# An interleaved attention pipeline: value loads asked for two turns ahead, bank-freeing steps first, new keys in the score bank

## The chip, the cores and the metric

The kernel runs on one core of a Trainium2 chip. TensorE (PE) multiplies matrices: a weight load (PEld) puts the stationary operand in place, a matmul streams the other one and writes PSUM, which has eight banks of 512 fp32 columns for each of the 128 partitions. VectorE (DVE), ScalarE (ACT) and GpSimd (POOL) do the elementwise work, and SyncE (SP) issues the DMAs to and from HBM. Each engine takes its instructions in order and waits on semaphores that other engines raise. The metric is the time of one launch on the device in microseconds.

## The reference, cut to what matters

Two layers of a streaming encoder are computed for a prompt of 512 frames and for 8 running streams of 16 frames each, 640 rows in all. Layer 0 has a feed-forward block (`ffn0`), a mixer of a complex state-space model beside stick-breaking attention (`mix0`), and a second feed-forward block; layer 1 has an SSD mixer between two feed-forward blocks. The change is inside the attention of `mix0`:

```python
def sb_block(q_blk, q_pos, k, v):
    z = jnp.einsum('bqhd,bkhd->bhqk', q_blk, k).astype(jnp.float32) * (SB_HEAD_DIM ** -0.5)
    mask = k_pos[None, :] < q_pos[:, None]
    sp = jnp.where(mask, jax.nn.softplus(z), 0.0)
    suffix = lax.cumsum(sp, axis=3, reverse=True) - sp
    w = jnp.where(mask, jnp.exp(jax.nn.log_sigmoid(z) - suffix), 0.0)
    return jnp.einsum('bhqk,bkhd->bqhd', w, v)
...
out = jnp.concatenate([s5_out, sb_out], axis=-1) @ w_out
```

There are 8 heads of 64. A prompt row sees the prompt rows before it; a row of a running stream sees 256 cached keys and values of its stream and the new rows before it.

## The kernel before, in words

**Units and turns.** The 8 heads go in four pairs `p`. Each pair has four units `u`: three cut up the prompt's causal triangle (`parts_of`, 512 or 384 score columns for each head), and `u == 3` is the running streams (384 columns: 128 of new keys, 256 of cached ones). The 16 units run as a pipeline of 16 turns, one unit a turn, in the loop `for s, (p, u) in enumerate(units)`. I number the turns 0 to 15, so turn 4p + u belongs to unit (p, u).

**What one unit needs.** `score` multiplies queries by keys into `z`, a PSUM tile of two banks (L1222, the mask by L1227; for the streams L1234, L1236 and L1239). `soft` on ACT makes softplus in three passes (L1246, then L83 twice). `sums` on DVE adds (L1256), runs the suffix sum as a scan (L1263) and subtracts (L1265). `expo` on ACT takes the exponential (L83 on `S`). `turn` on PE transposes the weights back into the same banks `z` (L1275), ACT copies them out to `es` (L1361), and `product` multiplies by the values (L1285; for the streams L1299 with the new values `vrev` and L1303 with the cached values `vc`). In turn `s` stand `turn(s)`, the copy L1361 of unit s, `expo(s + 1)`, `product(s)`, then `begin(s + 2)`, which gives `score(s + 2)`, then `soft(s + 2)` and `sums(s + 2)`. There are two `z` tiles.

**New keys.** The streams' score needs the pair's 128 new keys in reversed order. `new_keys(p)`, called by `begin` of unit (p, 1), takes a bank of the pool `a`, transposes the keys into it (L1203), copies them out (L1202), multiplies by a reversing matrix into the same bank (L1206) and copies that out (L1207), which ends in `kr[p]`.

**Values.** For unit (p, 3) `product` asks for four tiles `vc` of 256 KB, two for each half `f`, right at the matmuls that use them. There are three buffers.

**Fill.** Between the attention's own matmuls PE is given other work of the mixer: the projections of queries and keys of the next pairs, the gate of the state-space part and the first half of the output projection. They are `Group`s of 12 or 24 matmuls (L1021), each into one of three banks of the pool `a`. `fill(1.8)` stands between `turn` and `product`, `fill(3.2)` at the end of a turn; the figures are planned microseconds. A group starts only when the group three before it has been read out (`held[-3]`); before the change a `new_keys` counted as one of those holders. What reads a bank out are ACT steps (L1109 for queries and keys) or DVE steps (L1148 for the gate, L1184 for the output).

**Side work of ACT and DVE.** Steps that wait for their place are `Job`s in two lists. `slot(engine, us)` takes jobs that are ready from the front of the list until `us` is used up: casts of weights into a high and a low part (L1085, L1088), copies of activations into such parts (L1122, L1123), the gate's sigmoid (L83 on `gs`) and the readings of banks.

**What fixes the order.** From the mark before the pipeline to its end every PE, ACT and DVE instruction is chained to the one before it on its engine, so these three run in the order in which the code gives them. DMAs are not chained; the SP queue is laid out when the program is built. After the last turn the groups that are left run to their end, and then `out_half(4, t)` (L134) does the second half of the output projection.

## Time and profile before

| | |
|---|---|
| median of three runs | 2596.32 us (2596.07 to 2597.92) |
| the profiled execution's own time | 2597.03 us |
| its span, mean granted clock of PE | 2595.3 us, 0.988 |
| busy share of PEld, DVE, ACT, POOL | 89%, 78%, 47%, 11% |
| HBM traffic, mean over the span | 116 GB/s |
| the pipeline of 16 turns, with the groups left at its end | 568.65 to 757.97 us |
| `vc` loads: count, size, median time to landing | 16, 256 KB, 4.1 us |

A row of the timeline has the start, the duration, the engine, the line, the operation, what it writes and reads, the shape and how many instructions it merges; in brackets stands how long the engine was idle before it and what ended that. A row of the waits has the waiting engine, tile and line, what it waited for, then the total, the number of times and the longest. In a row of windows PEclk is the TensorE clock that was granted, as a share of full speed. Everything outside these 189 us is the same before and after the change.

### The profile page before, as it was taken

What the parts mean: (1) busy time and instruction counts of PE and PEld (TensorE: products, weight loads), DVE (VectorE), ACT (ScalarE), POOL (GpSimd) and SP (SyncE); (2) the same over time, 40 slices, a digit from 0 to 9 for tenths busy, and PEclk for the clock granted to TensorE, in tenths of its full rate; (3) what the DMA queues carried; (4) which work ended last, traced back from release to release, by engine and by line L of the source; (5) the groups of instructions that cost most, each with busy time, mean ns of one, the idle gap of its engine ahead of it and who ended that gap; (6) DMA issues with size and microseconds to landing.
All of it is one profiled execution on the core that took longest, in us unless ns stands there. A gap on an engine that the chain in (4) does not pass through costs nothing. (4 is left out here: it accounts for less than half of the span.)

```text
span 2595.3 us, 40664 instructions
## 1 busy us (share of the span) xinstructions
PE 2520.8 (97%) x15577; PEld 2303.1 (89%) x15577; DVE 2018.7 (78%) x3685; ACT 1226.3 (47%) x2329; POOL 285.4 (11%) x412
## 2 busy tenths in 40 slices
PE   8999999999799999999999999999999999999998
PEld 8999999878578999998999999889999878999997
DVE  7788877765657988887888887777777698876768
ACT  4443344346634454554355554566565443443332
POOL 0000002110011000003000001411111151000001
PEclk9999999999899999999999999999999999999999
DMA  5332334543211244443144335356564622443442
GB/s 181 106 106 81 115 111 140 169 134 108 87 53 49 66 126 110 110 126 107 57 110 115 106 93 164 89 181 182 179 199 136 232 95 77 153 153 113 142 137 94
DMA packets 174835, 317.44 MB, mean 122 GB/s; under 512 B 20480, under 2 KB 91776, under 8 KB 174128
## 3 DMA queue, kind: packets, MB, share of 16 engines
q1 hardware_dynamic: 164816, 293.83, 35.7%
q0 software_dynamic: 9824, 21.01, 3.9%
q8 instruction: 122, 2.00, 0.3%
q14 instruction: 73, 0.60, 0.1%
HBM read 259.56 MB, written 40.54 MB: 116 GB/s over the span
## 5 line engine op out<-in xcount | busy, mean ns | idle before, releaser
L96 DVE TENSOR_TENSOR w<-raw,w 128x512 fp32r<-128x512 f32 (+1 forms) x601 | 525.4, 899 | 78.3 <-ACT w L95 76.6
L95 ACT CAST w<-raw 128x512 fp32r<-128x512 f32 (+1 forms) x601 | 442.0, 776 | 297.1 <-PE bank L134 107.4
L356 PE MATMUL bank<-xhi,w 128*128 128x320 f32 x2432 | 540.1, 309 | 1.7 <-ACT mx L367 1.4
L134 PE MATMUL bank<-xhi,w 128*128 128x256 f32 (+2 forms) x2272 | 500.0, 312 | 14.5 <-ACT xhi L95 8.4
L134 PE MATMUL bank<-w,h 128*128 128x512 f32 x1872 | 435.3, 391 | 0.2 <-DVE w L96 0.2
L356 PE MATMUL bank<-T,w 128*128 128x320 f32 x2736 | 426.2, 309 | 2.0 <-DVE s L393 1.7
L134 PEld LDWEIGHTS bank<-w,h 128*128 128x128 f32 x1872 | 349.2, 188 | 72.9 <-DVE h L96 1.0
L356 PEld LDWEIGHTS bank<-xhi,w 128*128 128x128 f32 x2432 | 407.3, 188 | 5.9 <-ACT mx L367 2.8
L356 PEld LDWEIGHTS bank<-T,w 128*128 128x128 f32 x2736 | 406.4, 188 | 3.9 <-DVE s L393 2.2
L134 PEld LDWEIGHTS bank<-xhi,w 128*128 128x128 f32 x2272 | 379.6, 189 | 26.0 <-ACT xhi L95 9.6
L356 PE MATMUL bank<-xlo,w 128*128 128x320 f32 x1216 | 375.0, 308 | 0.0
L134 PE MATMUL bank<-xlo,w 128*128 128x256 f32 (+2 forms) x1136 | 351.9, 310 | 5.7 <-DVE xlo L96 5.7
L356 PEld LDWEIGHTS bank<-xlo,w 128*128 128x128 f32 x1216 | 228.0, 188 | 0.3
L134 PEld LDWEIGHTS bank<-xlo,w 128*128 128x128 f32 x1136 | 214.6, 189 | 7.6 <-DVE xlo L96 6.8
L209 DVE SCALAR_TENSOR_TENSOR yacc<-bank,yacc 128x512 f32<-128x512 f32 x160 | 109.4, 687 | 77.3 <-PE bank L134 76.7
L367 ACT COPY mx<-bank 128x320 f32<-128x320 f32 x228 | 96.3, 423 | 141.4 <-PE bank L356 140.6
L96 DVE TENSOR_TENSOR w<-sw,w 128x1024 fp32r<-128x1024 f32 x76 | 93.0, 1224 | 53.1 <-ACT w L95 52.8
L95 ACT CAST w<-sw 128x1024 fp32r<-128x1024 f32 x76 | 79.8, 1050 | 100.3 <-DVE sw L335 99.1
L500 POOL DMA_DIRECT2D yacc<-ev x56 | 48.6, 884 | 652.8 <-ACT ev L499 594.6
L134 PE MATMUL bank<-w,og 128*128 128x512 f32 x432 | 106.2, 400 | 3.5 <-DVE og L1769 3.5
L134 PEld LDWEIGHTS bank<-w,og 128*128 128x128 f32 x432 | 80.8, 191 | 21.5 <-DVE og L1769 5.1
L395 ACT ACTIVATE s<-s 128x320 f32<-128x320 f32 x108 | 50.8, 471 | 85.2 <-DVE s L393 85.0
(428 smaller groups left out, 3487.5 us busy)
## 6 DMA issues: line engine op xcount, KB each, us to landing
raw<-in_w_gate_dram SPq DMA_DIRECT2D x88, 512.0 KB, 3.8
raw<-in_w_up_dram SPq DMA_DIRECT2D x88, 512.0 KB, 4.0
raw<-in_w_down_dram SPq DMA_DIRECT2D x88, 512.0 KB, 3.6
raw<-in_m_in_dram SPq DMA_DIRECT2D x52, 512.0 KB, 4.6
yacc<-ev POOLq DMA_DIRECT2D x56, 256.0 KB, 4.1
raw<-in_m_out_dram SPq DMA_DIRECT2D x24, 512.0 KB, 3.8
csb<-cs_d SPq DMA_DIRECT2D x20, 512.0 KB, 5.0
h<-in_ssd_h_dram SPq DMA_DIRECT2D x16, 512.0 KB, 6.0
```

What stands on the lines that cost most here:

```text
L95: nc.scalar.copy(hi, src)
L96: return nc.vector.tensor_tensor(lo, src, hi.bitcast(F32), op=ALU.subtract)
L134: state["pe"] = nc.tensor.matmul(ps, a, b, start=(k == 0), stop=(k == n - 1)).ins
L209: state["acc"] = nc.vector.scalar_tensor_tensor(ya, pb, scale, ya, op0=ALU.mult, op1=ALU.add).ins
L356: nc.tensor.matmul(ps, A[p][:, a, k * 128:k * 128 + 128], B[p][b][:, k, :], start=(first and n == 0), stop=(n == 11), skip_group_check=True)
L367: nc.scalar.copy(e[n], ps)
L395: state["silu"] = nc.scalar.activation(t, ps, AF.Silu).ins
L500: nc.gpsimd.dma_start(yacc[:, t, 512 * j:512 * j + 512], e, accum_op=ALU.add)
```

## The change

1. The four `vc` tiles of unit (p, 3) are asked for in `begin` of that unit, which stands two turns ahead of its `product`, into four buffers instead of three.
2. Jobs that free a bank (what `Group.then` returns, and the first copy of the new keys) get `frees`, and `slot` takes these first.
3. `new_keys(p, z)` uses the 128 columns of each of unit (p, 1)'s two score banks that its 384 score columns leave over, instead of a bank of pool `a`: the transposition (now L1200) goes to columns 384 to 511 of the first, the reversed keys (now L1205) to those of the second. The copies are now L1201 and L1206. New keys no longer count among the holders of pool `a`.
4. The first `slot("act", 1.9)` of a turn becomes 2.6, the second 1.2.

```diff
@@ -964,7 +964,7 @@
             class Job:
 
                 def __init__(self, cost, give, needs=()):
-                    self.cost, self.give, self.needs, self.done = cost, give, list(needs), False
+                    self.cost, self.give, self.needs, self.done, self.frees = cost, give, list(needs), False, False
 
                 def ready(self):
                     return all(n.done for n in self.needs)
@@ -987,7 +987,7 @@
             def slot(engine, us):
 
                 while us > 0:
-                    todo[engine] = [j for j in todo[engine] if not j.done]
+                    todo[engine] = sorted((j for j in todo[engine] if not j.done), key=lambda j: not j.frees)
                     j = next((j for j in todo[engine] if j.ready()), None)
                     if j is None:
                         return
@@ -1022,6 +1022,7 @@
                                      skip_group_check=True)
                     if not self.left:
                         self.freed = self.then(self.ps)
+                        self.freed.frees = True
 
                 def run(self):
                     while not self.done:
@@ -1190,25 +1191,22 @@
 
             units = [(p, u) for p in range(4) for u in range(4)]
             parts_of = (((3, 0),), ((2, 0),), ((1, 0), (0, 256)))
-            ch, kr, po = {}, {}, {}
+            ch, kr, po, vals = {}, {}, {}, {}
             qbf = qb.rearrange("p f b h i -> p f (b h i)")
 
-            def new_keys(p):
+            def new_keys(p, z):
 
                 kk = wk.tile([128, 2, 128], F32, name="kk", bufs=2)
-                if len(held) > 2 and not held[-3].freed.done:
-                    held[-3].freed.run()
-                pk = bank_a()
-                first = later("act", 0.25, lambda: nc.scalar.copy(kk[:, 0], pk[:, 0:128]))
-                nc.tensor.transpose(pk[:, 0:128], qk[p, "k"][:, 512:640], ident)
+                nc.tensor.transpose(z[:, 0, 384:512], qk[p, "k"][:, 512:640], ident)
+                first = later("act", 0.25, lambda: nc.scalar.copy(kk[:, 0], z[:, 0, 384:512]))
+                first.frees = True
 
                 def turned():
-                    nc.tensor.matmul(pk[:, 128:256], kk[:, 0], anti, start=True, stop=True)
-                    nc.scalar.copy(kk[:, 1], pk[:, 128:256])
+                    nc.tensor.matmul(z[:, 1, 384:512], kk[:, 0], anti, start=True, stop=True)
+                    nc.scalar.copy(kk[:, 1], z[:, 1, 384:512])
 
                 kr[p] = Job(0.25, turned, [first])
-                kr[p].keys, kr[p].freed = kk[:, 1], kr[p]
-                held.append(kr[p])
+                kr[p].keys = kk[:, 1]
 
             def score(s):
                 p, u = units[s]
@@ -1238,6 +1236,8 @@
                         for j in range(4):
                             nc.tensor.matmul(z[32 * j:32 * j + 32, f, 128:384], qbf[:, f, 32 * j:32 * j + 32],
                                              kc[:, j, :], start=False, stop=(j == 3), skip_group_check=True)
+                if u == 1:
+                    new_keys(p, z)
                 ch[s] = [z[:, :, :n], wk.tile([128, 2, 512], F32, name="es", bufs=3)[:, :, :n], None]
 
             def soft(s):
@@ -1290,11 +1290,7 @@
                 wT = e.rearrange("p f (k r) -> p f k r", k=3)
                 ps = po[p, "s"] = bank("o")
                 for f in range(2):
-                    vcs = []
-                    for k in range(2):
-                        vc = wk.tile([128, 4, 128], F32, name="vc", bufs=3)
-                        nc.sync.dma_start(vc, I["vc"][p][:, 4 * f:4 * f + 4, k])
-                        vcs.append(vc)
+                    vcs = vals[p][2 * f:2 * f + 2]
                     o = slice(128 * f, 128 * f + 128)
                     nc.tensor.matmul(ps[:, o], wT[:, f, 0], vrev[:, 128 * p:128 * p + 128],
                                      start=(f == 0), stop=False, skip_group_check=True)
@@ -1325,13 +1321,17 @@
                             if p:
                                 made[p, n, h].run()
                 if u == 1:
-                    new_keys(p)
                     for h in range(2):
                         rows = slice(64 * h, 64 * h + 64)
                         nc.gpsimd.tensor_copy(qb[rows, :, :, h, :],
                                               qk[p, "q"][rows, 512:640].rearrange("p (f b i) -> p f b i", f=2, i=16))
-                if u == 3 and not kr[p].done:
-                    kr[p].run()
+                if u == 3:
+                    vals[p] = [wk.tile([128, 4, 128], F32, name="vc", bufs=4) for _ in range(4)]
+                    for f in range(2):
+                        for k in range(2):
+                            nc.sync.dma_start(vals[p][2 * f + k], I["vc"][p][:, 4 * f:4 * f + 4, k])
+                    if not kr[p].done:
+                        kr[p].run()
                 score(s)
 
             for p in (1, 2, 3):
@@ -1359,7 +1359,7 @@
                     fetch(order[len(raws)])
                 turn(s)
                 nc.scalar.copy(ch[s][1], ch[s][0])
-                slot("act", 1.9)
+                slot("act", 2.6)
                 fill(FILL[0])
                 if s + 1 < len(units):
                     expo(s + 1)
@@ -1381,7 +1381,7 @@
                     sums(s + 2)
                 if u == 0:
                     kr[p].run()
-                slot("act", 1.9)
+                slot("act", 1.2)
                 fill(FILL[1])
                 if (p, u) == (3, 2):
                     split_x(7, qk[3, "q"], 0, TP, [made[3, n, h] for n in "qk" for h in range(2)])
```

Lines below line 1190 move up by two to four: L1222, L1227, L1239, L1303 and L1184 are L1220, L1225, L1237, L1299 and L1185 in the changed program; those near L1100 move down by one.

**SP, the loads around the pair p = 1.** `raw` are weights, `kc` cached keys, `out_kT` a result. Before:

```order
L1075 DMA raw<-in_m_out_dram 128x1024 x2
L1233 DMA kc<-in_kcT_dram 128x1024 x2
L1111 DMA out_kT_dram<-kT 128x640
L1075 DMA raw<-in_m_out_dram 128x1024
L1296 DMA vc<-in_vc_dram 128x4x128 x2
```

After:

```order
L1231 DMA kc<-in_kcT_dram 128x1024 x2
L1112 DMA out_kT_dram<-kT 128x640
L1076 DMA raw<-in_m_out_dram 128x1024
L1332 DMA vc<-in_vc_dram 128x4x128 x3
L1076 DMA raw<-in_m_out_dram 128x1024
L1332 DMA vc<-in_vc_dram 128x4x128
```

Before, the two `vc` at this place are the fourth of pair 0 and the first of pair 1, each behind the matmuls that free one of the three buffers; after, the `vc` at this place are all four of pair 1.

**PE, around the first transposition (turn 0).** Before:

```order
L1021 MATMUL bank<-xlo,w 128x256
L1275 MATMUL bank<-ident,S 128x128 x8
L1285 MATMUL bank<-es,vt 64x128 x8
L1222 MATMUL bank<-kT,qT 128x256 x2
L1222 MATMUL bank<-kT,qT 128x128 x2
```

After:

```order
L1021 MATMUL bank<-xlo,w 128x384
L1021 MATMUL bank<-xhi,w 128x384
L1275 MATMUL bank<-ident,S 128x128 x8
L1021 MATMUL bank<-xhi,w 128x384
L1021 MATMUL bank<-xlo,w 128x384
```

A third group of 24 matmuls of 384 columns now starts here, since no new keys hold a bank: 10 of them stand ahead of the transposition and 11 between it and the product.

**ACT, from the softplus of unit (2, 1) to the copy of turn 8.** Before (the copies of the new keys are L1202 and L1207):

```order
L1246 ACTIVATE es<-bank 128x2x384
L83 ACTIVATE es<-es 128x2x384 x2
L1122 CAST xhi<-g_4561 128x384
L1122 CAST xhi<-g_4562 128x384
L1122 CAST xhi<-g_4563 128x384
L1122 CAST xhi<-g_4564 128x384
L1361 COPY es<-bank 128x1024
```

After:

```order
L1246 ACTIVATE es<-bank 128x2x384
L83 ACTIVATE es<-es 128x2x384 x2
L1201 COPY kk<-bank 128x128
L83 ACTIVATE gs<-gs 128x256 x3
L1361 COPY es<-bank 128x1024
```

The first copy of the new keys now stands ahead of the copy L1361 of turn 8, with a sigmoid (`gs`) between. It reads a bank that DVE reads too, and in the changed program it waits for DVE's subtraction L1265 on that bank (for the pairs 1 to 3; for pair 0 it stands ahead of DVE's pass). The matmul L1205 has the same wait, for all four pairs.

**ACT, from the softplus of unit (2, 3) to the copy of turn 10, after the change:**

```order
L1246 ACTIVATE es<-bank 128x2x384
L95 CAST w<-raw 128x512
L83 ACTIVATE es<-es 128x2x384
L95 CAST w<-raw 128x512
L83 ACTIVATE es<-es 128x2x384
L1123 CAST xhi<-g_4563 128x256
L1123 CAST xhi<-g_4564 128x256
L83 ACTIVATE gs<-gs 128x384 x3
L1361 COPY es<-bank 128x2x384
```

Before, six sigmoid steps of 256 columns stood between the last pass of the softplus and the copy of this turn, and no cast.

## The prediction

> **What bounds the kernel now.** I read the page's first two parts first, then windows around the 16 turns, then PE's waits there, then the timelines of the turns in which it waits.
>
> ```profile
> span 2595.3 us, 40664 instructions
> PE 2520.8 (97%) x15577; PEld 2303.1 (89%) x15577; DVE 2018.7 (78%) x3685; ACT 1226.3 (47%) x2329; POOL 285.4 (11%) x412
> ```
>
> PE is busy for 97% of the span, so only its 75 us of idle time and the time at a low clock can be won without taking work away. The windows below take the pipeline as a whole and then in three parts, turns 0 to 6, turns 7 (its end) to 12, and the rest.
>
> ```profile
> core 0: us, PE busy (x) PEld busy (x) DVE busy (x) ACT busy (x) POOL busy (x), PEclk, DMA share, GB/s
> 568.65:757.97 189.32, 159.76 (x1119) 127.55 (x1118) 106.54 (x156) 109.41 (x178) 2.90 (x8) 0.89 0.26 81
> 568.65:652.41 83.76, 77.58 (x596) 65.14 (x595) 48.08 (x62) 52.26 (x79) 1.16 (x4) 0.94 0.31 100
> 652.41:718.68 66.27, 47.67 (x317) 36.43 (x318) 39.73 (x64) 44.50 (x77) 0.58 (x2) 0.79 0.28 84
> 718.68:757.97 39.29, 34.52 (x208) 25.98 (x206) 18.74 (x32) 12.65 (x23) 1.16 (x2) 0.96 0.10 36
> ```
>
> The pipeline takes 189.3 us. PE is idle for 189.3 - 159.8 = 29.6 us of it, and a mean clock of 0.89 loses up to 0.11 x 189.3 = 20.8 us more (5.0, 13.9 and 1.6 by its three parts; what of it falls on idle time costs nothing). The middle part is the worst, with 18.6 us idle. No other engine is full there: ACT has 44.5 of 66.3 us, DVE 39.7. So PE waits for answers, not for an engine's throughput.
>
> ```profile
> PE bank L1303 <- DMA vc<-in_vc_dram: 10.3, 4, 4.1
> PE bank L1285 <- ACT es L1361: 6.0, 3, 4.0
> PE bank L1021 <- ACT kT L1109: 4.1, 1, 4.1
> PE bank L1206 <- ACT kk L1202: 2.8, 1, 2.8
> PE bank L1275 <- ACT S L83: 2.5, 1, 2.5
> PE bank L1021 <- DVE yacc L1184: 1.2, 1, 1.2
> PE bank L134 <- DVE yacc L1184: 1.2, 1, 1.2
> PE bank L1021 <- DVE gs L1148: 0.6, 1, 0.6
> PE bank L1311 <- ACT pvs L1307: 0.5, 1, 0.5
> PE bank L1299 <- ACT es L1361: 0.4, 1, 0.4
> ```
>
> These ten rows add up to the 29.6 us.
>
> **Part 1, the values: 10.3 us go.** The last eight matmuls of each streams' product wait for a load.
>
> ```profile
> 695.49 5.81 SPq L1296 DMA_DIRECT2D vc<-in_vc_dram  x4
> 700.21 0.66 PE L1303 MATMUL bank<-vc,es 128*32 128x128 f32 x8 [4.12 <-DMA vc<-in_vc_dram]
> ```
>
> With three buffers the fourth tile can be asked for only when the product has read the first one, and part of the load (4.1 us to landing, the median of the 16) then lies bare on PE. With four buffers all four are asked for once the previous pair's product is through, some 30 us ahead; the two results and weight loads that stand before them on SP wait for steps of earlier turns. Nothing is late in their place: the cached keys have had their buffers before. All 10.3 us go.
>
> **Part 2, banks: the other 19.3 us go, some comes back.** A third group starts early, and readings of banks come first. In turn 0:
>
> ```profile
> 581.48 1.10 PE L1275 MATMUL bank<-ident,S 128*128 128x128 f32 x8 [2.49 <-ACT S L83]
> 583.67 1.97 PE L1285 MATMUL bank<-es,vt 128*64 128x128 f32 x16 [1.10 <-ACT es L1361]
> 590.25 0.51 PE L1021 MATMUL bank<-xhi,w 128*128 128x384 f32 x2
> 590.77 0.51 PE L1021 MATMUL bank<-xhi,w 128*128 128x384 f32 x2
> ```
>
> Three matmuls of 384 columns take 0.52 us start to start, so ten ahead of the transposition cover 1.7 us of the first wait and eleven behind it the whole second one; about 1.0 us is left. The wait for L1109 (4.1) goes, since that step no longer stands behind four copies; the one for L1206 (2.8) goes, since the copy it waits for now stands ahead of an L1361 that PE has waited for by then. The waits for DVE's `yacc` (2.4) go: five matmuls are left at the end instead of 51, and the bank of the first L134 has then long been read. The product's waits in turns 9 and 12 (4.9 of the 6.0) are priced anew in parts 3 and 4.
>
> **Part 3, the new keys: a new wait for ACT.** No row of before shows ACT waiting with the copy of the keys, for they had a bank of their own. In the program after, L1201 waits for L1265, DVE's last pass over the score bank; behind it in ACT's queue stands L1361, for which PE's product waits. The nearest rows are those of turn 4:
>
> ```profile
> 616.90 0.39 PE L1227 MATMUL bank<-negc,identb 128*128 128x128 bf16 x2
> 617.33 0.81 ACT L1246 ACTIVATE es<-bank 128x768 f32<-128x768 f32 x1 [1.11 <-PE bank L1227]
> 618.17 1.72 ACT L83 ACTIVATE es<-es 128x768 f32<-128x768 f32 x2
> 620.06 0.26 ACT L1202 COPY kk<-bank 128x128 f32<-128x128 f32 x1
> 619.92 0.96 DVE L1256 SCALAR_TENSOR_TENSOR es<-bank,es 128x768 f32<-128x768 f32 x1 [1.50 <-ACT es L83]
> 622.76 0.96 DVE L1265 TENSOR_TENSOR S<-bank,S 128x768 f32<-128x768 f32 x1
> 622.00 1.04 PE L1275 MATMUL bank<-ident,S 128*128 128x128 f32 x8
> 623.07 1.02 ACT L1361 COPY es<-bank 128x1024 f32<-128x1024 f32 x1 [2.75 <-PE bank L1275]
> ```
>
> From the score's end to the end of L1361 it will be 2.6 (three passes of ACT) + 3.8 (619.92 to 623.72 on DVE) + 0.26 + 1.02 + about 0.3 of hand-overs = 7.9 us. Meanwhile PE has streams_back with a wait for `pvs` (0.8), the fill of 3.2 planned (19 matmuls, 3.3), the transposition (0.8) and the fill of 1.8 planned (1.9): 6.8. So turn 4 waits 1.2 us. In turn 8 a sigmoid of three passes stands between (1.25) and only two matmuls fill between transposition and product (0.35): 7.9 + 1.25 - 5.4 = 3.8. In turn 12 two copies stand between (1.2): 7.9 + 1.2 - 6.8 = 2.3. Sum **7.3**. Bounds: nothing, if PE is late for other reasons and the pass is over; 3 x (3.8 + 0.26 + 1.0) = 15.2, if all of pass and copies lies bare. I take the middle, which the rows of turn 4 give.
>
> **Part 4, ACT's jobs in turns 9 and 10.** More sigmoids and casts stand ahead of the copy for the product than before.
>
> ```profile
> 681.71 2.51 ACT L83 ACTIVATE gs<-gs 128x256 f32<-128x256 f32 x6
> 690.56 0.60 ACT L95 CAST w<-raw 128x512 fp32r<-128x512 f32 x1
> 694.10 0.71 ACT L1122 CAST xhi<-g 128x256 fp32r<-128x256 f32 x2
> 717.15 1.64 ACT L83 ACTIVATE gs<-gs 128x384 f32<-128x384 f32 x3
> 684.12 0.78 ACT L1361 COPY es<-bank 128x768 f32<-128x768 f32 x1
> 710.40 1.98 PE L1285 MATMUL bank<-es,vt 128*64 128x128 f32 x16 [3.99 <-ACT es L1361]
> ```
>
> Turn 10: from the score's end 2.6 + two casts 1.2 + two copies 0.7 + a sigmoid 1.64 + L1361 0.8 = 6.9; PE has six matmuls (1.05) and the transposition (0.6), as no further group can start: it waits 5.3. Turn 9: 2.6 + 1.2 + 0.25 (second copy of keys) + 2.5 + 0.8 = 7.3 against 0.2 + 3.3 + 0.6 + 1.9 = 6.0: it waits 1.3. Sum **6.6**; bounds nothing and 6.9 + 7.3 = 14.2. The last row shows such a wait in turn 12 of before (3.99), of the same kind. The larger first `slot` (2.6 for 1.9) stands behind L1361 of its own turn and ahead of the next exponential, which PE needs only some 5 us later; I price it at nothing (at most 16 x 0.7 = 11 us if that cover went).
>
> **The sum.** Idle: 29.6 goes; 7.3 + 6.6 + 1.0 (turn 0) + 2.0 (four waits for `pvs`, 0.5 each as in the row of L1311) + 0.6 (DVE's bank readings, as now) = 17.5 comes: 12.1 saved. The matmuls moved forward from the end are no saving of their own, they fill this. Clock: in the middle part 13.9 us are lost beside 18.6 idle, 0.75 for each idle us; by that rate the five new stalls and turn 0, 13.9 + 1.0 = 14.9 us, lose 11.2 instead of 20.5: 9.3 saved. Together 21.4 us off the profiled execution's own 2597.0 (span and what lies around it), which is 0.7 over the median of the runs: **2575 us** as a median, 0.8% less.
>
> **A rule on the clock.**
>
> ```profile
> 615.35 0.42 PE L1303 MATMUL bank<-vc,es 128*32 128x128 f32 x8 [2.08 <-DMA vc<-in_vc_dram]
> 617.00:618.00 1.00, 1.00 (x6) 0.50 0.94 357
> 620.00:621.00 1.00, 1.00 (x7) 0.96 0.00 0
> ```
>
> A stall of 2.08 us was followed by half clock from about 616.8 to 620.1, 3.3 us, or 1.6 us lost. The Trainium skill ("TensorE: Matmul & The Clock Gate", Part 1) says the clock halves after an idle window of some 3.4 us, in windows that run freely. The window's length agrees with the trace, the idle time needed doesn't: 2.08 us were enough.
>
> **Rivals.**
>
> *A, only long stalls cost clock.* If just the two longest stalls (turns 8 and 10, 3.8 and 5.3) halve it, for one window of 3.3 us each, 3.3 us are lost instead of 11.2: 2567 us. For it: turns 0 to 6 lose only 5.0 us of clock. Against: the 2.08 above. The Trainium skill, on the page and in the part named above, gives a limit of some 3.4 us, which lies between 2.08 and 3.8.
>
> *B, the chain of answers was the bound, not the banks.* A turn cannot be shorter than score, softplus, DVE's pass, exponential, transposition and copy let it; matmuls put between then only hide what was hidden, and the product waits as long as before. Then only the values' 10.3 us are won: 2586 us. For it: ACT and DVE hand over five times within a turn. Against: turns 0 to 6 have 83.8 - 77.6 = 6.2 us idle, turn 0's 3.6 and one load's 2.1 among them, so the other turns run without a wait where there is fill.
>
> *C, slower.* The hold of L1201 blocks ACT in turns 4, 8 and 12 and delays the score behind the product, so the next softplus and DVE's pass start late and the delay rolls on through turns 9 to 13. Each us of stall costs 1.75 with its clock, so the sign turns once the five stalls (turns 4, 8, 9, 10, 12) together exceed 13.9 + 21.4 / 1.75 = 26 us, 5.2 each. At 6.5 each they are 18.6 over my sum, and the time is 2575 + 33 = 2608 us. For it: in the program after, the wait is on the whole of DVE's pass, not on the columns that are read. Against: ACT has a third of that part free (44.5 of 66.3). The Trainium skill ("PSUM — Partial Sum Buffer", PSUM bank collisions raise a hardware error) says that two engines must not be at one bank and quadrant together even at different columns, two readers included; so by it the spare columns can't be read while DVE is at the bank; no run here shows a collision.
>
> *D, the loads come no earlier.* SP works in order; were the values to stay behind a weight load that waits for its buffer, the 10.3 us and some 5 of clock would stay: 2590 us. Against: the order, in which they stand behind steps of earlier turns.
>
> **How the numbers follow.** Forecast 0.57, A 0.13, B 0.14, C 0.07, D 0.05; within 0.2% of before (5 us, about what a measurement of this kernel can tell from no change) 0.04 more. Faster gathers the forecast, A, B and most of D: 0.87; the same 0.06; slower 0.07. The unknown prices move the forecast by 7.3 + 6.6 = 14 downwards (no such stall, 2561) and by 7.9 + 7.6 = 15 upwards (2590), so the range of 2561 to 2590 takes in A, B and D and leaves out C.
>
> **What would show it.** The waits of L1303 for a DMA: none. The first L1275: 1.0 us of wait. L1201 idle before it for 3 us or more in three turns, released by L1265. The product of turn 10 waiting about 5 us, turn 8 about 4. Five matmuls L1021 between L1307 and L134. A mean clock of 0.93 to 0.94 over the pipeline, which is about 168 us long. Wrong would be a wait for `vc` left, product waits over 20 us together, or a pipeline over 180 us.

## The result, and the profile after

The changed kernel takes **2571.62 us** (median of 4 runs, 2568.28 to 2576.97), against 2597.12 us (2596.07 to 2599.11, 4 runs) of the kernel before on the same chip: a ratio of 0.9903, 95% interval 0.9884 to 0.9922. Forecast were 2575 us. The profiled execution took 2573.02 us, 24.0 less than the profiled one of before.

The first rows are the span and the engines from the page; then the windows, the pipeline as a whole and its three parts with turns 0 to 6, the middle, and the rest (columns as in the rows of before).

```profile
span 2571.3 us, 40672 instructions
PE 2511.2 (98%) x15577; PEld 2297.1 (89%) x15577; DVE 2017.1 (78%) x3685; ACT 1225.1 (48%) x2329; POOL 287.3 (11%) x412
```

```profile
572.02:736.34 164.32, 148.06 (x1120) 119.54 (x1119) 107.04 (x155) 108.28 (x175) 3.35 (x8) 0.96 0.28 87
572.02:652.41 80.39, 77.15 (x637) 65.17 (x636) 49.78 (x66) 55.06 (x86) 1.16 (x4) 1.00 0.35 115
652.41:713.41 61.00, 48.74 (x324) 37.91 (x325) 42.70 (x68) 43.15 (x75) 1.03 (x2) 0.89 0.26 78
713.41:736.34 22.93, 22.17 (x163) 16.46 (x161) 14.56 (x23) 10.06 (x15) 1.16 (x2) 1.00 0.05 14
```

The pipeline is 25.0 us shorter (189.3 to 164.3). Two terms make this up: PE is idle for 164.3 - 148.1 = 16.3 us of it instead of 29.6, which is 13.3 less, and the same matmuls keep it busy for 148.1 instead of 159.8, which is 11.7 less, since more of them run at full clock. Ahead of the pipeline this execution lost 3.4 us (it starts at 572.02, before at 568.65), which the last section takes up. Behind it it won 2.4; this I did not follow up, but the two executions of one kernel below, e10_no_frees and c2_no_frees, differ there by 4.7 us (1839.7 and 1835.0 us from the pipeline's end to the span's), so it is no more than chance makes.

PE's waits in the pipeline, first all of them, then one by one from the timeline:

```profile
PE bank L1285 <- ACT es L1361: 12.9, 5, 4.9
PE bank L1307 <- ACT pvs L1303: 1.1, 2, 0.6
PE bank L1275 <- ACT S L83: 1.0, 1, 1.0
PE bank L1021 <- ACT kT L1110: 0.6, 1, 0.6
PE bank L1275 <- ACT kk L1206: 0.4, 1, 0.4
PE bank L1021 <- DVE yacc L1185: 0.3, 1, 0.3
```

```profile
584.85 1.09 PE L1275 MATMUL bank<-ident,S 128*128 128x128 f32 x8 [1.00 <-ACT S L83]
624.31 0.88 PE L1285 MATMUL bank<-es,vt 128*64 128x128 f32 x12 [1.01 <-ACT es L1361]
662.47 1.97 PE L1285 MATMUL bank<-es,vt 128*64 128x128 f32 x16 [4.01 <-ACT es L1361]
673.66 0.88 PE L1285 MATMUL bank<-es,vt 128*64 128x128 f32 x12 [0.66 <-ACT es L1361]
683.39 1.55 PE L1285 MATMUL bank<-es,vt 128*64 128x128 f32 x12 [4.87 <-ACT es L1361]
706.00 1.58 PE L1285 MATMUL bank<-es,vt 128*64 128x128 f32 x16 [2.35 <-ACT es L1361]
```

No row waits for a load any more. What is left is nearly all the product's wait for L1361, in turns 4, 8, 9, 10 and 12. In turn 8 the timelines of ACT, and under it of DVE, show why:

```profile
655.34 0.85 ACT L83 ACTIVATE es<-es 128x768 f32<-128x768 f32 x1
660.04 0.27 ACT L1201 COPY kk<-bank 128x128 f32<-128x128 f32 x1 [3.85 <-DVE S L1265]
660.21 1.31 ACT L83 ACTIVATE gs<-gs 128x256 f32<-128x256 f32 x3
661.43 0.99 ACT L1361 COPY es<-bank 128x1024 f32<-128x1024 f32 x1
```

```profile
656.22 0.96 DVE L1256 SCALAR_TENSOR_TENSOR es<-bank,es 128x768 f32<-128x768 f32 x1 [0.32 <-ACT es L83]
657.21 1.81 DVE L1263 TENSOR_TENSOR_SCAN S<-onec,es 128x384 f32<-128x384 f32 x2
659.05 0.96 DVE L1265 TENSOR_TENSOR S<-bank,S 128x768 f32<-128x768 f32 x1
```

ACT stands still for 3.85 us with the copy of the new keys, until DVE has ended its last pass over the score bank (L1265, at 659.05 + 0.96), and L1361 and with it PE's product stand behind it. In turns 4 and 12 the same hold takes 3.48 and 3.86.

### The profile page after: what moved, and what is told of

Read it like the earlier page. It is cut to its first block, busy times and chain, and to the rows that moved or that the text cites. A ratio compares the mean times of both kernels' runs of the same rounds, so it can differ in the third digit from the quotient of the medians.

```text
span 2571.3 us, 40672 instructions
## 1 busy us (share of the span) xinstructions
PE 2511.2 (98%) x15577; PEld 2297.1 (89%) x15577; DVE 2017.1 (78%) x3685; ACT 1225.1 (48%) x2329; POOL 287.3 (11%) x412
## 5 line engine op out<-in xcount | busy, mean ns | idle before, releaser
L134 PE MATMUL bank<-xhi,w 128*128 128x256 f32 (+2 forms) x2272 | 502.5, 313 | 14.5 <-ACT xhi L95 8.2
L134 PE MATMUL bank<-w,h 128*128 128x512 f32 x1872 | 435.1, 390 | 0.0
L134 PEld LDWEIGHTS bank<-w,h 128*128 128x128 f32 x1872 | 349.2, 188 | 72.5 <-DVE h L96 1.0
L134 PEld LDWEIGHTS bank<-xhi,w 128*128 128x128 f32 x2272 | 382.2, 190 | 26.1 <-ACT xhi L95 9.5
L134 PE MATMUL bank<-xlo,w 128*128 128x256 f32 (+2 forms) x1136 | 353.8, 312 | 5.8 <-DVE xlo L96 5.8
L134 PEld LDWEIGHTS bank<-xlo,w 128*128 128x128 f32 x1136 | 215.9, 190 | 7.7 <-DVE xlo L96 7.0
L134 PE MATMUL bank<-w,og 128*128 128x512 f32 x432 | 104.9, 396 | 3.0 <-DVE og L1769 2.8
L134 PEld LDWEIGHTS bank<-w,og 128*128 128x128 f32 x432 | 79.6, 188 | 21.0 <-DVE og L1769 4.6
```

Of the source, the lines that this page charges most:

```text
L134: state["pe"] = nc.tensor.matmul(ps, a, b, start=(k == 0), stop=(k == n - 1)).ins
```

## The experiments

All twelve, with the two kernels themselves. The ratio is to the kernel before on the same chip, with its 95% interval; the pipeline's length, PE's waits in it (length less PE's busy time) and the pieces of half clock in it are from each profiled execution. A piece is 3.4 us long (see the run that spreads the fill).

| kernel | median us | ratio | pipeline us | waits us | pieces |
|---|---|---|---|---|---|
| before | 2597.12 | 1 | 189.3 | 29.6 | 12 |
| the change | 2571.62 | 0.9903 (0.9884 to 0.9922) | 164.3 | 16.3 | 4 |
| e1_values: values alone | 2582.59 | 0.9943 (0.9930 to 0.9955) | 172.4 | 21.5 | 5 |
| e2_keys: keys alone | 2581.72 | 0.9939 (0.9926 to 0.9953) | 171.8 | 21.3 | 5 |
| e3_frees: bank steps first alone | 2588.68 | 0.9962 (0.9949 to 0.9974) | 179.2 | 23.8 | 10 |
| e4_slots: slots alone | 2596.66 | 0.9997 (0.9988 to 1.0006) | 187.0 | 29.5 | 10 |
| e5_no_values: the change without values | 2580.16 | 0.9936 (0.9923 to 0.9948) | 174.2 | 20.4 | 8 |
| e6_no_keys: without keys | 2570.14 | 0.9892 (0.9878 to 0.9905) | 164.5 | 15.6 | 4 |
| e10_no_frees: without bank steps first | 2567.86 | 0.9882 (0.9868 to 0.9896) | 158.4 | 13.9 | 2 |
| c1_change: the change again | 2572.20 | 0.9907 (0.9891 to 0.9922) | 163.5 | 16.2 | 4 |
| c2_no_frees: without bank steps first, again | 2567.87 | 0.9889 (0.9873 to 0.9906) | 159.8 | 14.2 | 2 |
| e7_keys_ahead | 2563.39 | 0.9862 (0.9848 to 0.9875) | 154.0 | 10.1 | 1 |
| e8_small_jobs | 2558.79 | 0.9851 (0.9838 to 0.9865) | 152.1 | 7.4 | 2 |
| e9_spread | 2559.58 | 0.9849 (0.9835 to 0.9863) | 150.8 | 8.0 | 0 |

My theory was the sum of the prediction; the rivals were that the values alone pay (B), and that the parts only work together.

### One part at a time

**e1_values** is the kernel before with part 1 of the change:

```diff
-                    vcs = []
...
+                    vcs = vals[p][2 * f:2 * f + 2]
...
+                if u == 3:
+                    vals[p] = [wk.tile([128, 4, 128], F32, name="vc", bufs=4) for _ in range(4)]
```

> The kernel before with change 1 alone (values asked for two turns ahead, four buffers); PE's order of matmuls is that of before. Theory (the forecast's term): the 10.3 us of waits for the values go, the other 19.3 us of the pipeline's waits stay, and with the four stalls of 4 us or less their low clock goes, 0.4 to 0.75 us for each: 2597 - 10.3 - (4 to 8) = 2579 to 2583. Rival (the time is only handed on: behind each product the next transposition waits for ACT's or DVE's answer instead): the waits of PE in the pipeline come to 25 us or more and the time is 2590 or more.

Measured: 2582.59 us, as the theory has it. No wait for a load is left; the rest of the waits is that of before within 1 us each. The pipeline is 16.9 us shorter: the 10.3 of the loads go, 2.2 of small waits elsewhere come, and PE's busy time falls by 8.8, with five pieces of half clock in place of twelve.

**e2_keys** has part 3 alone:

```diff
-                pk = bank_a()
-                first = later("act", 0.25, lambda: nc.scalar.copy(kk[:, 0], pk[:, 0:128]))
-                nc.tensor.transpose(pk[:, 0:128], qk[p, "k"][:, 512:640], ident)
+                nc.tensor.transpose(z[:, 0, 384:512], qk[p, "k"][:, 512:640], ident)
+                first = later("act", 0.25, lambda: nc.scalar.copy(kk[:, 0], z[:, 0, 384:512]))
```

> The kernel before with change 3 alone (new keys in spare score columns). In the program this alone moves nearly all of the filling matmuls as the whole change does: eleven in place of none behind the transposition of turn 0, and five in place of 51 left at the end. Theory: the waits of turn 0, for the copy of the keys and for yacc go (8.8 us), the waits for the values stay (10), and turns 4, 8, 10 and 12 wait for ACT as after the whole change (about 12): PE's waits in the pipeline come to 25 to 29 us, so 2587 to 2596 with a clock not worse than before. Rival (the new keys' place carries the whole gain, the rest is covered by it): 2577 or less. Rival (the held-up ACT costs more than the bank brings): 2600 or more.

Measured: 2581.72 us, below the 2587 to 2596 that I had expected and above the rival's 2577. Turn 0 came out as forecast (1.0 of wait), the values still cost 8.4, but turn 8 had no wait for L1361 at all. Without part 2 the copy of turn 8's keys isn't taken first, and stands behind L1361. So in turn 8 the hold needs part 2 as well. In turns 4 and 12 part 3 alone makes it: ACT's copy of the keys waits 3.48 and 3.46 us for DVE's last pass there, and the product 1.35 and 0.88. The runs without part 2 follow this up.

**e3_frees** has part 2 alone:

```diff
-                    todo[engine] = [j for j in todo[engine] if not j.done]
+                    todo[engine] = sorted((j for j in todo[engine] if not j.done), key=lambda j: not j.frees)
...
+                        self.freed.frees = True
...
+                first.frees = True
```

> The kernel before with change 2 alone (steps that free banks given first; the keys keep a bank of their own). In the program, eight or nine of the filling matmuls of turn 12 go to places elsewhere, 28 in place of 51 are left at the end, and turn 0 has none behind its transposition, as before. Theory: the waits for L1109's step (4.1), for yacc (part of 2.4) and for the copy of the keys go, turn 0's 3.6 and the values' 10.3 stay, and turns 8 and 11, with no matmuls between transposition and product, wait some 3 us each: waits of 22 to 26 us, 2588 to 2594. Rival (order of the bank steps is what the gain hangs on): 2582 or less.

Measured: 2588.68 us, and 23.8 us of waits, as the theory has both. The places were others: turn 8 waited 1.1, and turn 11 5.6 (for L1361) and 2.9 (for the values).

**e4_slots** has part 4 alone:

```diff
-                slot("act", 1.9)
+                slot("act", 2.6)
...
-                slot("act", 1.9)
+                slot("act", 1.2)
```

> The kernel before with change 4 alone (the two slots for ACT's jobs 2.6 and 1.2 in place of 1.9 and 1.9). PE's order is that of before; a few casts, weight casts and sigmoids move on ACT past the copy for the product. Theory (the forecast's term): priced at nothing, since ACT has a third of the pipeline free and the larger slot stands ahead of an exponential that PE needs later; the wait for L1109's step (4.1) may change, since what stands ahead of it does: 2592 to 2600. Rival (smaller second slots shorten the copies that PE waits for): 2590 or less, with the 6.0 us of product waits falling below 3. Rival (the larger first slot holds up the exponential): 2602 or more, with new waits of the transpositions for ACT's S.

Measured: 2596.66 us, ratio 0.9997 with an interval on both sides of 1: nothing clear of the noise, as priced. The waits are those of before; the 2.3 us by which this execution's pipeline is shorter go with two pieces of half clock fewer (10 in place of 12), and the medians, 0.7 us apart, don't show them.

### The change without one part

**e5_no_values** is the change with the values asked for where they are used, in three buffers again:

```diff
-                    vcs = vals[p][2 * f:2 * f + 2]
+                    vcs = []
+                    for k in range(2):
+                        vc = wk.tile([128, 4, 128], F32, name="vc", bufs=3)
...
```

> The changed kernel without change 1 (values asked for where they are used, three buffers). Theory: four waits for the values come back, 8 to 10 us, and with them two to four low-clock windows of 3.3 us (1.7 us each), less what turn 12's wait for ACT (2.35) gives back: 2571.6 + 12 = 2581 to 2587. Rival (values and banks overlap: the wait for the load takes the place of ACT's waits): 2578 or less.

Measured: 2580.16 us, a little under the theory's 2581. The waits for values came back (8.5 us) with four more pieces of half clock, and turns 8 and 12 waited 2.35 and 1.36 in place of 4.0 and 2.35; I take it that ACT and DVE get on while PE waits for the load of the turn before. Three of the four parts without the values win 17 us, so rival B falls.

**e6_no_keys** is the change with the keys in a bank of pool `a`:

```diff
+                pk = bank_a()
...
-                nc.tensor.transpose(z[:, 0, 384:512], qk[p, "k"][:, 512:640], ident)
+                nc.tensor.transpose(pk[:, 0:128], qk[p, "k"][:, 512:640], ident)
```

> The changed kernel without change 3 (the new keys keep a bank of their own; values early, bank-freeing steps first and slots as in the change). PE's order is that of the run of change 2 alone. Theory (the forecast's parts 2 and 3): turn 0's waits (3.6 against 1.0) come back with a clock window or two, turn 12's matmuls move elsewhere, and ACT no longer waits for L1265, so turns 4, 8 and 12 lose 7.4 us of product waits; the run of change 2 alone had 23.7 us of waits in the pipeline, 8.7 of them for values, so 14 to 16 us are left, as many as after the whole change (16.3): 2570 to 2576. Rival (the keys' place carries the gain, the other three do not add up without it): 2580 or more.

Measured: 2570.14 us, in the range of the theory. The new place of the keys, worth 17.5 us of pipeline alone (e2_keys), is worth 0.2 on top of the other three, and the medians (2570.14 against 2571.62, with ratios whose intervals overlap) show no gain either: it takes away turn 0's waits (3.6 to 1.0) and turn 11's (5.6), and brings or lengthens those of turns 4, 8, 10 and 12.

**e10_no_frees** is the change without part 2; **c1_change** and **c2_no_frees** are the change and this kernel once more, side by side on one chip:

```diff
-                    todo[engine] = sorted((j for j in todo[engine] if not j.done), key=lambda j: not j.frees)
+                    todo[engine] = [j for j in todo[engine] if not j.done]
...
-                        self.freed.frees = True
...
-                first.frees = True
```

> The changed kernel without change 2 (steps that free banks take their turn with the others). PE's order is that of the change; on ACT the step for kT of turn 6 stands behind four casts again, and the new keys of turn 8 are copied behind the copy for the product. Theory (change 2 pays only where the keys have a bank): the product of turn 8 no longer waits behind the hold (4.0 go), the keys' matmul in turn 9 waits instead (2.9 come, as in the run of change 3 alone), and kT's wait grows by about 1: 2569 to 2575 against 2571.6. Rival (change 2 carries its own 8 us here too): 2577 or more.

> The whole change once more, beside the next kernel on the same chip. Theory: the pipeline takes 164 us again with the same waits and a median of 0.989 to 0.991 of before. Rival (the profiled execution was a chance draw): waits of turns 8, 10 and 12 that differ by over 1 us from 4.0, 4.9 and 2.4.

> The change without change 2 once more, beside the whole change on the same chip. Theory (change 2 with change 3 puts the copy of the new keys ahead of the product's copy, and its hold costs more than the earlier banks bring): 3 to 6 us less than the whole change. Rival (the two are the same, and the trace's 158 against 164 us of the pipeline is a matter of where the low-clock pieces fell): within 2 us.

Measured: 2567.86 us, a little under the 2569 expected, and side by side 2567.87 (2565.75 to 2569.49) against 2572.20 (2570.37 to 2576.99): no run of the one reaches the other. So beside the other three parts, part 2 *costs* 4.3 us. The whole change was itself again: a pipeline of 163.5 us and waits of 4.02, 4.87 and 1.95 in turns 8, 10 and 12, where the first execution had 4.01, 4.87 and 2.35. ACT's timeline of turn 8 without it:

```profile
654.15 1.30 ACT L83 ACTIVATE gs<-gs 128x256 f32<-128x256 f32 x3
655.36 0.60 ACT L1085 CAST w<-raw 128x512 fp32r<-128x512 f32 x1
656.10 1.01 ACT L1359 COPY es<-bank 128x1024 f32<-128x1024 f32 x1
657.00 0.62 ACT L1085 CAST w<-raw 128x512 fp32r<-128x512 f32 x1
657.52 1.32 ACT L83 ACTIVATE gs<-gs 128x256 f32<-128x256 f32 x3
658.75 0.25 ACT L1200 COPY kk<-bank 128x128 f32<-128x128 f32 x1
```

Compared with the rows above, the copy of the keys (here L1200) stands behind the product's copy (here L1359) and waits for nothing; the product's wait is 0.76 in place of 4.01. In turns 4 and 12 the hold stays without part 2 (here L1263 is DVE's last pass):

```profile
619.45 0.27 ACT L1200 COPY kk<-bank 128x128 f32<-128x128 f32 x1 [3.48 <-DVE S L1263]
696.15 0.27 ACT L1200 COPY kk<-bank 128x128 f32<-128x128 f32 x1 [3.46 <-DVE S L1263]
```

The product's waits fall by 5.2 us in all (12.9 to 7.7). What part 2 wins is less: 1.6 at kT's step (2.2 without it, 0.6 with it) and 1.4 at a reading of a bank by DVE (L1148), a wait that the change doesn't have. With the small ones the waits are 2.4 us fewer, and the rest of the gain is clock (two pieces in place of four). I had expected the keys' own matmul to wait 2.9 in turn 9, as in e2_keys; it didn't.

### The hold taken away

**e7_keys_ahead** copies the keys right behind the softplus, ahead of DVE's pass:

```diff
-                kr[p].keys = kk[:, 1]
+                kr[p].keys, kr[p].first = kk[:, 1], first
...
                     soft(s + 2)
+                    if units[s + 2][1] == 1:
+                        kr[units[s + 2][0]].first.run()
```

> The changed kernel, but ACT copies the new keys right behind the three softplus passes over the same score bank, so ahead of DVE's pass and not behind it. PE's order of matmuls is that of after. Theory (the hold of L1201 for L1265 is what the product waits for in turns 4, 8 and 12): their waits, 1.0, 4.0 and 2.4 us, go or fall under 1 us each, that of turn 10 (4.9) stays, and with some 3 us of clock the time is 2561 to 2566 against 2571.6. Rival (the chain from softplus over DVE to the exponential sets it, the copy only stood in its shade): the transposition of turn s+1 or DVE's L1254 now waits as long, and the time is 2570 to 2574. Rival (the copy ahead of DVE delays DVE's pass and thereby the next transposition): 2575 or more.

Measured: 2563.39 us, ratio 0.9862, as the theory has it. These are PE's products of turns 8, 9 and 10; turns 4 and 12 have no wait at L1285 at all:

```profile
656.44 1.09 PE L1285 MATMUL bank<-es,vt 128*64 128x128 f32 x16 [0.74 <-ACT es L1361]
666.00 0.88 PE L1285 MATMUL bank<-es,vt 128*64 128x128 f32 x12 [1.07 <-ACT es L1361]
675.73 1.30 PE L1285 MATMUL bank<-es,vt 128*64 128x128 f32 x12 [4.87 <-ACT es L1361]
```

Turn 10's wait stays to the hundredth, as it should if it comes from ACT's other jobs.

### Turns 9 and 10

**e8_small_jobs** adds to this smaller jobs ahead of the product's copy:

```diff
-                slot("act", 2.6)
+                slot("act", 3.2)
...
-                slot("act", 1.2)
+                slot("act", 0.6)
```

> The kernel with the keys copied ahead of DVE's pass, and its slots for ACT's jobs 3.2 and 0.6 in place of 2.6 and 1.2, so that in turns 8 to 11 fewer sigmoids stand ahead of the copy for the product: in turn 10 two casts and no sigmoid of 384 columns (1.6 us), in turn 9 two sigmoids of 256 columns fewer behind the weight casts (up to 1.6). PE's order is unchanged. Theory (the forecast's part 4: ACT's queue ahead of L1361 sets the waits of turns 9 and 10): 4.87 falls to 3.2, 1.07 to nothing, and 2.5 us are won against 2563.4: 2560 to 2562. Rival (DVE's pass or the transposition comes last there, the sigmoid stood in its shade): waits and time as they were, 2562 to 2565. Rival (the sigmoids moved behind it hold up the next softplus): waits of turns 11 and 12 appear, 2566 or more.

Measured: 2558.79 us, ratio 0.9851, just under the theory's range. Turn 10's row is

```profile
670.78 1.55 PE L1285 MATMUL bank<-es,vt 128*64 128x128 f32 x12 [3.61 <-ACT es L1361]
```

and turn 9 has no wait. The sigmoid of 1.63 us in front of L1361 was worth 1.26 of turn 10's 4.87, and the 1.07 of turn 9 went. In turn 10 the softplus, two weight casts and two copies still stand on ACT ahead of L1361, without a gap, while PE has only six matmuls and the transposition.

### The clock

**e9_spread** holds back 12 matmuls of fill in turns 8 and 9 for turn 10:

```diff
-                fill(FILL[0])
+                fill(0.9 if s == 9 else FILL[0])
...
-                fill(FILL[1])
+                fill(2.0 if s == 8 else FILL[1])
```

> The kernel with keys ahead and small jobs, and 12 of the filling matmuls of turns 8 and 9 held back, so that 18 in place of 6 stand ahead of turn 10's transposition; the same matmuls in all. In the ten traces so far the half clock comes in pieces that start on a grid of 3.413 us, and comes after every piece of full clock in which PE was idle for 1.8 us or more. Theory (the clock is lost by idle time within one piece, not by idle time in all): turn 10's wait of 3.6 falls to 0.3 to 1.5, turn 9 gets one of up to 1.6, and with no piece that has 1.8 us idle the two half-clock pieces (1.7 us each) go: 2558.8 - 3.4 - about 1 = 2554 to 2556. Rival (clock is lost at a rate for each us of waiting): waits of 6 to 7 us in the pipeline against 7.4 and half-clock pieces as before: 2557 to 2559. Rival (weight casts and sigmoids that come later hold up the out-projection's groups): waits for ACT or DVE at L1021 in turns 11 and 12, 2560 or more.

Measured: 2559.58 us, ratio 0.9849 against 0.9851 of e8_small_jobs: the same within the intervals, in the range of neither theory. The trace decides between them. The windows over the pipeline, of e8_small_jobs and then of e9_spread:

```profile
567.58:719.72 152.14, 144.79 (x1119) 117.25 (x1119) 106.32 (x155) 107.80 (x175) 2.97 (x8) 0.98 0.30 94
```

```profile
569.23:720.06 150.83, 142.80 (x1120) 115.71 (x1119) 106.19 (x155) 107.71 (x175) 3.11 (x8) 1.00 0.30 95
```

PE waits 0.7 us *more* (8.0 against 7.4), but no wait is over 1.1, no piece of half clock is left, and the same matmuls take 2.0 us less: idle time in small parts costs no clock. The two pieces had been worth 2.0, not the 3.4 that I had expected. PE was busy for 2.49 and 3.42 us in them, so half speed should have cost 3.0; where the other 1.0 went I didn't follow up. The 1.3 us that remain are too few for the medians to show. This and e8_small_jobs are the fastest kernels of the study, 12 and 13 us below the change.

## Why the prediction was right

The forecast of 2575 was 3.4 us too high, with the sign and the mechanism right, and one term, the clock, mis-sized. By its own steps:

1. **Values, 10.3 us go.** Right: no load is waited for, after the change and in e1_values. Rival D falls with this.
2. **Turn 0, 1.0 left.** 1.00. The waits for kT's step (L1109, now L1110) and `yacc` go from 4.1 and 2.4 to 0.6 and 0.3, the keys' matmul waits no more (2.8), and the first L134 doesn't wait.
3. **The new wait for ACT, 7.3 in turns 4, 8 and 12** (1.2, 3.8 and 2.3). 1.01, 4.01 and 2.35, together 7.4. (By its own terms the chain is 8.0 and not 7.9, and PE's work in turn 8 is 5.25 and not 5.4, so the forecast for that turn should have read 4.0.) ACT is idle ahead of L1201 for 3.48, 3.85 and 3.86 us until L1265. e7_keys_ahead takes the hold away and these waits all but go (0.74 in turn 8 is left). That the largest of the three, turn 8's, needs part 2 beside part 3 was not in the forecast, though the sum had both.
4. **ACT's jobs, 6.6 in turns 9 and 10** (1.3 and 5.3). 1.03 (0.66 at the product, and 0.37 at the transposition for the second copy of the keys, where the forecast had no wait) and 4.87, and e8_small_jobs shows them to be ACT's queue, in part. The slots by themselves: nothing that the medians show, as priced.
5. **Idle time 17.5.** 16.3; the waits for `pvs` came to 1.1 instead of 2.0.
6. **Clock, 9.3 saved.** This is the term that was mis-sized. PE's busy time fell by 11.7. The forecast took the loss as 0.75 us for each idle us, a rate from a stretch with stalls of 2.1 to 4.1 us one behind the other, and so 11.2 us for the five new stalls and turn 0. In fact turns 0, 4 and 9 cost no clock at all, and turns 8, 10 and 12 brought four pieces of 3.4 us at half speed. PE was busy for 12.4 us of them, so they cost 6.2. The loss before was mis-sized too: the forecast took all 20.5, though it says itself that what falls on idle time costs nothing. In the twelve pieces of before PE was busy for 35.1 of 41.0 us, which is 17.5 lost. 17.5 - 6.2 = 11.3 agrees with the 11.7 but for 0.4. So one error of 3.0 and one of 5.0 partly cancelled in the forecast's 9.3, which is luck. Together 13.3 + 11.7 = 25.0, where the forecast had 21.4; the medians are 25.5 apart. For the same reason the pipeline took 164.3 us at a mean clock of 0.96, where 168 at 0.93 to 0.94 had been expected.

Rival A had the right idea for the small stalls and the wrong count for the large ones: two pieces, 3.3 us, where turn 12's wait of 2.35 us cost a piece too and turn 10's cost two. Rival C needed the five stalls to exceed 26 us together; they were 1.0 + 4.0 + 1.0 + 4.9 + 2.4 = 13.3, and nothing rolled on.

How large each part is depends on what stands beside it: alone they shorten the pipeline by 16.9, 17.5, 10.1 and 2.3 us, 46.8 in all, together by 25.0 (by the medians 16.2, 17.0, 10.1 and 0.7, together by 25.5). Keys and bank steps cure in part the same wait: that for kT's step (4.1) goes with the one and falls to 1.3 with the other.

## What to carry to other kernels

When a copy moves into a bank that another engine is about to pass over, look where it stands in its engine's queue: ahead of that pass it costs 0.3 us here, behind it the queue stands still for 3.5 to 3.9, and a rule that "frees a bank first" can put it exactly there, as in turn 8. Measure each part of a change alone and left out, since two cures for one wait don't add up, and one of them may cost. And spread the idle time that can't be removed: several waits of 1 us cost just themselves, one of 4 us costs up to two pieces of half clock more. The traces show this; between e8_small_jobs and e9_spread it was too little for the medians to tell.

## What the runs showed of the hardware

**The half clock comes in pieces on a grid.** Windows over the changed kernel, 3.413 us each, around the stalls of turns 8, 10 and 12:

```profile
658.67:662.08 3.41, 0.00 (x0) 0.00 (x0) 2.12 (x4) 1.97 (x5) 0.00 (x0) 1.00 0.00 0
662.08:665.49 3.41, 3.02 (x22) 2.52 (x24) 2.46 (x5) 3.35 (x8) 0.00 (x0) 0.50 0.18 18
665.49:668.91 3.42, 3.42 (x27) 3.30 (x24) 1.10 (x2) 2.51 (x4) 0.00 (x0) 1.00 0.37 143
...
679.15:682.56 3.41, 0.00 (x0) 0.00 (x0) 2.76 (x5) 3.35 (x8) 0.00 (x0) 1.00 0.64 196
682.56:685.97 3.41, 2.58 (x16) 1.65 (x16) 2.73 (x4) 3.35 (x7) 0.00 (x0) 0.50 0.24 97
685.97:689.39 3.42, 3.42 (x12) 2.03 (x9) 2.30 (x6) 2.09 (x3) 0.00 (x0) 0.50 0.01 2
689.39:692.80 3.41, 3.41 (x20) 2.86 (x19) 2.21 (x2) 2.87 (x6) 0.00 (x0) 1.00 0.00 0
...
703.04:706.45 3.41, 1.06 (x11) 0.63 (x11) 3.06 (x5) 2.71 (x5) 0.00 (x0) 1.00 0.00 0
706.45:709.87 3.42, 3.42 (x26) 2.69 (x23) 0.00 (x0) 0.37 (x2) 0.00 (x0) 0.50 0.00 0
```

The first column of numbers behind the length is PE's busy time, the third from the right the granted clock. Within an execution all pieces lie on one grid of 3.413 us (from 662.08 to 682.56 are six steps, to 706.45 seven more), and a piece is full or half as a whole. A piece in which PE was idle for long is followed by one of half clock. Over the pipelines of all 14 traces, from a piece at full clock: with 2.0 us idle or more the next was half in each of 38 cases, with less than 1.5 in none, and between the two in 7 of 15. My figure of 1.8 us in the text ahead of e9_spread was too sharp: 1.93 once passed (e10_no_frees). Within half clock 0.7 us idle or more was followed by another half piece each time, as at 682.56; four times a half piece followed on less, once on none at all (e6_no_keys, 686.11), which I can't explain. The changed kernel's second execution, c1_change, had four pieces as well, but two behind turn 8, two behind turn 10 and none behind turn 12. The Trainium skill ("TensorE: Matmul & The Clock Gate", Part 1) gives the same 3413 ns and says that the window runs freely. The length agrees with the trace to the digit. Its condition, at least one idle window, doesn't: here 2.0 of 3.4 us were enough.

**So the same wait costs nothing, one piece or two, by chance.** Some 100 us ahead of the pipeline, in code that the change leaves alone, PE waits 2.7 to 2.8 us for DVE. On the grid of each execution, before and then after:

```profile
466.49:469.90 3.41, 1.86 (x12) 1.30 (x10) 2.65 (x7) 1.33 (x3) 0.00 (x0) 1.00 0.89 264
469.90:473.32 3.42, 2.01 (x11) 2.01 (x12) 1.89 (x7) 0.00 (x0) 0.00 (x0) 1.00 1.04 364
473.32:476.73 3.41, 3.41 (x21) 3.41 (x21) 0.26 (x1) 1.29 (x3) 0.00 (x0) 1.00 1.00 400
```

```profile
467.53:470.94 3.41, 1.51 (x9) 0.95 (x7) 2.36 (x8) 1.04 (x2) 0.00 (x0) 1.00 0.88 254
470.94:474.35 3.41, 2.24 (x7) 2.25 (x8) 1.64 (x5) 0.00 (x0) 0.00 (x0) 0.50 1.05 395
474.35:477.77 3.42, 3.42 (x13) 3.42 (x12) 0.00 (x0) 0.00 (x0) 0.00 (x0) 0.50 0.95 378
```

Before, the wait fell on two pieces, 1.55 and 1.41 us idle, and nothing followed; after, 1.90 fell into one, in the band where either happened, and two half pieces came. PE was busy for 2.24 and 3.42 us in them, so 2.8 us were lost. With 0.5 us by which this execution was late already (at the transposition L196, 460.28 against 459.78), this makes up the 3.4 us by which the pipeline began later, but for 0.1. Of the 14 executions eight have one or two half pieces at this place and six have none, with the same code. So this is likely to be one source of the spread of runs (2568 to 2577 after), though only one execution of each run was traced; and it is why a difference of 2 us between two kernels here needs the trace.
